# A decoder layer on one Trainium2 core: the softmax division is moved from the probabilities to the output of each pair of heads

## The chip, the core and the metric

The kernel runs on one core of one Trainium2 chip. Five engines work side by side, each through its own queue in order: TensorE (PE, matmuls and transposes), VectorE (DVE), ScalarE (ACT), GpSimd (POOL) and SyncE (SP), which here issues the DMA transfers. The metric is the device time of one execution in microseconds; less is better.

## The reference, cut to what matters

One layer of a hybrid decoder, 512 tokens of width 1024 in float32: a norm, one combined input projection, sparse attention (16 heads of 64) beside a state-space mixer, a gated merge, an output projection, a gated MLP and a last norm. The change touches the attention alone:

```python
def block(args):
    qb, qib, wib, blk = args
    ...
    _, sel = lax.top_k(score, n_sel)
    c_sel = gather(c_kv, sel)
    logits = jnp.einsum("bqhc,bqkc->bhqk", qb, c_sel,
                        preferred_element_type=jnp.float32) * scale
    ...
    logits = jnp.where((dist >= 0)[:, None], logits, -jnp.inf)
    p = jax.nn.softmax(logits, axis=-1).astype(c_sel.dtype)
    return jnp.einsum("bhqk,bqkc->bqhc", p, c_sel)
```

Each query of a head divides its exponentials by their sum. The division may stand before the product with the values or after it, since the sum belongs to the row.

## The kernel before

The kernel keeps float32 accuracy by splitting every operand into a high and a low part (the helper `split`: ACT copies the high part, another engine subtracts to get the low one) and multiplying high by high, high by low and low by high. Weights come in as tiles wr of 512 KB, are split into wh (ACT, L86) and wl (POOL, L87), and two wr buffers are used in turn.

Attention is one loop over h from 0 to 17. A pass writes out, woven together by the helper `weave`: the logits and the softmax of head h, the transposes of the probabilities of head h−1, the product of head h−2 with the values, in every fourth pass the values' projection V (`v_step`), and fillers for PE (projections of the next pairs, gates). Two heads make a pair p, whose output is one tile of 128 partitions, 64 for each head. In a pass:

- `logits` (L720 to L762): a table T of the relative bias is loaded (L726); POOL adds it to the mask into bm (L730, L731, L737), which has one buffer; PE computes the logits of the four query blocks into pl, and DVE adds bm and takes the row maximum (L747) into pr and mx. `soft` lets ACT take the exponentials with the sums in sm (L754), DVE the reciprocals (L756), and DVE scale the four blocks of pr (L759).
- `ptrans` (L764 to L781): PE transposes pr in 128 by 128 blocks (L775, the tile pPT), ACT copies the high part (PTh, L778) and DVE the low part (PTl, L779).
- `pav_` (L785 to L801): PE multiplies with the values V (L794). The result's rows of the head and its low part lie on different halves of the partitions. ACT copies one half into the tile ath (L799), a DMA brings it to the other half into atl (L800), and DVE copies the rest into cr (L801), which has one buffer for all pairs.
- `att_split` (L804 to L808): cr is completed by adding atl (L807), and split into ath (ACT, L86) and atl (L87). POOL does the add and the subtraction for pairs 0 to 5, DVE for 6 and 7.

The order within each engine isn't that of the text: a scheduler moves instructions. In the built program `att_split` of pair p stands on POOL in the pass of the odd head 2p+3, behind the four bm additions. After the loop come the two gates' and the attention's output projections, pga and pao (L105), and the merge; pao needs ath and atl of all eight pairs.

PE's queue, ACT's and DVE's hold the steps of several heads in turn, so a late step holds all that stands behind it on its engine.

Of the kernel before, what the change touches and what calls it, by code (L numbers as in the profile page):

```python
# [9 lines left out]
F32 = mybir.dt.float32  # L10
R32 = mybir.dt.float32r
AF = mybir.ActivationFunctionType
OP = mybir.AluOpType

P = 128
S = 512
# [32 lines left out]
def _body(ctx, tc, x, prm_d, cst_d, nfin_d, wI_d, wX_d, wSO_d, wQ_d, wG_d, wAO_d, wO_d, wUp_d, wDn_d,  # L49
# [18 lines left out]
    def f(t):  # L68
        return t.bitcast(F32)
# [12 lines left out]
    ident = cv("ident")  # L82

    def split(hi, lo, src, lo_eng=None):
        """hi = fp32r(src), lo = fp32r(src - hi)."""
        nc.scalar.activation(hi, src, AF.Copy)  # L86
        (lo_eng or nc.vector).tensor_tensor(lo, src, f(hi), OP.subtract)  # L87

# [10 lines left out]
        return hi, lo  # L99

    def mm3(ps, terms):
        """ps = sum of lhs.T @ rhs over terms of ((lhs_hi, lhs_lo), (rhs_hi, rhs_lo))."""
        seq = [(a[0], b[0]) for a, b in terms] + [(a[0], b[1]) for a, b in terms] + [(a[1], b[0]) for a, b in terms]
        for i, (l, r) in enumerate(seq):
            nc.tensor.matmul(ps, l, r, start=(i == 0), stop=(i == len(seq) - 1))  # L105

    def rsqrt(dst, ss, scale, eps, n, pool):
        """dst = (ss*scale + eps)^-0.5"""
        t = pool.tile([P, n], F32, tag="rsq", name="rsq")
        nc.vector.tensor_scalar(t, ss, scale, eps, OP.mult, OP.add)  # L110
        nc.gpsimd.tensor_tensor(dst, t, mhalf[:, :n], OP.pow)
# [5 lines left out]
            for k in range(KD)]  # L117

    def norm_T(xts, gname, dst, pool, sq, scl):
        """dst = rmsnorm(xts).T in hi and lo; sq and scl: the engine (ACT or DVE) of each block's squares and scaling."""  # L120
        for hf in range(2):
            alloc = mmt if hf == 0 else cht
            ps = [alloc(f"nT{gname}{hf}{i}").rearrange("p (k n) -> p k n", k=2) for i in range(KD // 2)]
            for bb in range(2):
                b = 2 * hf + bb
                xn = pool.tile([P, D], F32, tag="xn", name=f"xn{gname}{b}", bufs=4)
                ss = pool.tile([P, 1], F32, tag="nss", name=f"nss{gname}{b}", bufs=4)
                rs = pool.tile([P, 1], F32, tag="nrs", name=f"nrs{gname}{b}", bufs=4)
                if sq[b] == "v":
                    nc.vector.scalar_tensor_tensor(xn, xts[b], 1.0, xts[b], OP.mult, OP.mult, accum_out=ss)  # L130
                else:
                    nc.scalar.activation(xn, xts[b], AF.Square, accum_out=ss)
                rsqrt(rs, ss, 1.0 / D, EPS, 1, pool)
                if scl[b] == "a":
                    nc.scalar.activation(xn, xts[b], AF.Copy, scale=rs)
                else:
                    nc.vector.tensor_scalar(xn, xts[b], rs, None, OP.mult)
                for k in range(KD):
                    nc.tensor.transpose(ps[k // 2][:, k % 2, bb * P:(bb + 1) * P], xn[:, k * P:(k + 1) * P], ident)
            hs = slice(hf * 256, (hf + 1) * 256)  # L140
            for k in range(KD):
                g = pv(gname, k, k + 1)
                p_ = ps[k // 2][:, k % 2, :]
                nc.scalar.activation(dst[k][0][:, hs], p_, AF.Copy, scale=g)  # L144
                nc.vector.scalar_tensor_tensor(dst[k][1][:, hs], p_, g, f(dst[k][0][:, hs]), OP.mult, OP.subtract)
# [6 lines left out]
    def proj_T(ps, w):  # L152
        mm3(ps, [((w[0][:, k * P:(k + 1) * P], w[1][:, k * P:(k + 1) * P]), actT[k]) for k in range(KD)])

# [1 line left out]
    mid_stack = ExitStack()  # L156
    mid = mid_stack.enter_context(tc.tile_pool(name="mid", bufs=1, side="right"))
    ckvT = (mid.tile([P, S], R32, tag="ckh", name="ckh"), mid.tile([P, S], R32, tag="ckl", name="ckl"))
# [16 lines left out]
    with tc.tile_pool(name="n1", bufs=2) as n1:  # L175
# [15 lines left out]
        nc.sync.dma_start(cs1, cst_d[:, NKEEP:])  # L191
        norm_T(xts, "gmix", actT, n1, "vava", "aavv")

# [1 line left out]
        ps = mmt("pkidx")  # L195
        psc = mmt("pcr")
        for hf in range(2):
# [33 lines left out]
            nc.scalar.activation(ckvT[0], pk, AF.Copy)  # L231
            nc.vector.tensor_tensor(ckvT[1], pk, f(ckvT[0]), OP.subtract)

# [1 line left out]
        dx = dtS.rearrange("p a b -> p (a b)")  # L235
        e = n1.tile([P, 128], F32, tag="sp_e", name="sp_e", bufs=1)
        z = n1.tile([P, 128], F32, tag="sp_z", name="sp_z", bufs=1)
# [35 lines left out]

        latent()

# [1 line left out]
        pu = cht("pu")  # L277
        nc.tensor.matmul(pu[:H, :UW], pv("relb")[:BUCKETS, :], oh, start=True, stop=True)
        us = n1.tile([H, UW], F32, tag="us", name="us", bufs=1)
        nc.vector.tensor_copy(us, pu[:H, :UW])  # L280
        nc.sync.dma_start(uD, us)

# [1 line left out]
    nc.vector.tensor_copy(msk[:, 0:P], cv("maskc"))  # L284
    sds = ExitStack()
    sd = sds.enter_context(tc.tile_pool(name="sd", bufs=2))

    def dup_q(ps, name, tags, pool, scale, bufs):
        """Per head of a pair, its rows hi and lo on both halves of the partitions."""
        out = []  # L290
        for hh in range(2):
            r, o = slice(64 * hh, 64 * hh + 64), slice(64 - 64 * hh, 128 - 64 * hh)
            hi = pool.tile([P, S], R32, tag=tags[2 * hh], name=f"{name}h{hh}", bufs=bufs)
            lo = pool.tile([P, S], R32, tag=tags[2 * hh + 1], name=f"{name}l{hh}", bufs=bufs)
            nc.scalar.activation(hi[r], ps[r], AF.Copy, scale=scale)
            nc.vector.scalar_tensor_tensor(lo[r], ps[r], scale, f(hi[r]), OP.mult, OP.subtract)
            nc.sync.dma_start(f(hi[o]), f(hi[r]))
            nc.sync.dma_start(f(lo[o]), f(lo[r]))
            out.append((hi, lo))
        return out  # L300
# [37 lines left out]
            out += [lambda r=rnd, k=k: r(k=k) for k in range(16)]  # L338
        return out

# [1 line left out]
    def weave(chain, fill):  # L342
        """Emit the chain's (weight, step)s in order, the fillers spread between them by weight."""
        total = sum(w for w, _ in chain) or 1
        acc = done = 0
        for w, step in chain:
# [7 lines left out]
            fill[k]()  # L354

    def proj_steps(name, wsrc, after, parts=2):
        """One column tile of a projection of actT, in emission steps."""
        st = {}

        def seq():  # L360
# [287 lines left out]
    prev[0]()  # L648
    last_trans, so_last = prev[1:]

# [1 line left out]
    attT = []  # L652
    ao_stack = ExitStack()

# [16 lines left out]
            wkv.append((hi, lo))  # L671

    qTs, kTs, Vs, prs, PTs = {}, {}, {}, {}, {}
    KOF = (0, 512, 1024, 896)

    def v_step(qd):
# [44 lines left out]
    def logits(h):  # L721
# [28 lines left out]
        def soft():  # L750
# [3 lines left out]
                nc.scalar.activation(pr[:, o:o + n], pr[:, o:o + n], AF.Exp, bias=mx[:, i:i + 1],  # L754
                                     accum_out=sm[:, i:i + 1])
            nc.vector.reciprocal(sm, sm)  # L756
            for i in range(NB):
                o, n = SEG[i], (i + 1) * P
                nc.vector.tensor_scalar(pr[:, o:o + n], pr[:, o:o + n], sm[:, i:i + 1], None, OP.mult)  # L759
            prs[h] = pr  # L760

        return [lambda i=i: lg(i) for i in range(NB)] + [soft]  # L762
# [20 lines left out]
    crs = {}  # L783

    def pav_(h):  # L785
        """Even heads: [Vh|Vl], odd heads: [Vl|Vh], so that the low part lands on the other half of the partitions."""
        p, hh = h // 2, h % 2
        r, o_ = slice(64 * hh, 64 * hh + 64), slice(64 - 64 * hh, 128 - 64 * hh)
        V, PT = Vs[p // 2], PTs[h]
# [9 lines left out]
        nc.scalar.activation(hi[o_], pav[o_], AF.Copy)  # L799
        nc.sync.dma_start(f(lo[r]), f(hi[o_]))  # L800
        nc.vector.tensor_copy(crs[p][r], pav[r])  # L801

    def att_split(p):
        hi, lo = attT[p]  # L804
        s_ = crs[p]
        eng = nc.vector if p >= 6 else nc.gpsimd
        eng.tensor_tensor(s_, s_, f(lo), OP.add)  # L807
        split(hi, lo, s_, lo_eng=eng)  # L808

    sds.close()  # L810
# [44 lines left out]
        weave(chain, fl)  # L855
    att_split(7)

# [1 line left out]
    at.close()  # L859
    nxs = ExitStack()  # L860
    nx = nxs.enter_context(tc.tile_pool(name="nx", bufs=1, side="right"))
# [15 lines left out]
        split(hi, lo, tg)  # L877
        mg.append((hi, lo))

# [1 line left out]
    x1 = [big.tile([P, D], F32, tag=f"ys{b}", name=f"x1{b}") for b in range(NB)]  # L881
    for b in range(NB):
        nc.sync.dma_start(x1[b], x[b * P:(b + 1) * P, :])
# [120 lines left out]


def _coltile(w):
    """(K, N) -> (N/128, 128, K/128 * 128): per column tile, rows on partitions."""
    k, n = w.shape
    return np.ascontiguousarray(w.reshape(k // P, P, n // P, P).transpose(2, 1, 0, 3)).reshape(n // P, P, k)

# [75 lines left out]
```

## Time and profile before

| | us |
|---|---|
| three runs of the kernel before | 1187.9, 1189.9, 1190.06 |
| their median | 1189.9 |
| span of the profiled execution | 1188.0 |
| attention stage within it, first to last scaling | 525.6 to 677.9 |
| PE busy, share of the span | 1113.1, 94% |
| DVE busy | 705.9, 59% |
| ACT busy | 582.3, 49% |
| POOL busy | 518.0, 44% |
| granted clock of PE, most slices | 0.9 or more of full |

The profiled execution is one more run of the same program; only its span is known, from the first instruction to the last. The runs' times are some microseconds above a span, since they hold what lies around it. The share of busy time is a mean over stages with different limits, so each statement on the change has to be read from the attention stage alone.

### The profile page before, as it was taken

To read this page: it belongs to the slowest core of one execution; us is meant where nothing else is said; L and a number is where in the kernel's file an instruction comes from. 1 tells how busy PE (TensorE), PEld (TensorE's weight loads), DVE (VectorE), ACT (ScalarE), POOL (GpSimd) and SP (SyncE) were. 2 spreads that over 40 slices of the span, in tenths; PEclk is the share of its full clock that TensorE was granted. 3 is DMA by queue.
4 is the path that set the end of the run, shared out by engine and by line. 5 is a ranking of instruction groups with operands and counts; after the bars stand their busy time and mean duration, and the time that the engine had idled before them with its cause. 6 is when DMAs were issued, how large, how long until landed. Compare 5 with 4: busy or idle time off the path is not lost.

```text
span 1188.0 us, 14616 instructions
## 1 busy us (share of the span) xinstructions
PE 1113.1 (94%) x5268; PEld 920.8 (78%) x5268; DVE 705.9 (59%) x1324; ACT 582.3 (49%) x942; POOL 518.0 (44%) x287
## 2 busy tenths in 40 slices
PE   5898996998999889899999899999999999999997
PEld 5677775876887678778878788888888888888885
DVE  5569999998579689368988833305533344330004
ACT  5356464557476555456667633215444444432113
POOL 3324343334524434566566444444444444444442
PEclk9989999999999899999999999999999999999999
DMA  5264322222322231443434133232332222222221
GB/s 186 90 184 143 107 81 80 89 87 74 116 80 83 86 116 59 122 127 107 129 102 125 47 110 123 107 110 86 106 106 90 104 91 99 97 89 107 89 105 73
DMA packets 43306, 122.06 MB, mean 103 GB/s; under 512 B 5393, under 2 KB 9761, under 8 KB 43233
## 3 DMA queue, kind: packets, MB, share of 16 engines
q1 hardware_dynamic: 42656, 120.07, 30.5%
q8 instruction: 42, 0.69, 0.2%
q10 hardware_dynamic: 576, 1.05, 0.2%
q14 instruction: 32, 0.25, 0.1%
HBM read 108.29 MB, written 5.32 MB: 96 GB/s over the span
## 4 chain that ended last, share of the span: by engine, by line
PE 57%; DVE 26%; ACT 5%; issue 3%; POOL 2%; DMA 2%; POOLq 0%; DVEq 0%; ACTq 0%
PE pup L105 20%; PE pdn L947 10%; PE pso L464 5%; PE pao L105 4%; PE pga L105 4%; PE pwo L891 3%; DVE dec L524 3%; DVE u L388 3%; PE pxbc L373 3%; DVE msk L333 2%; DVE dec L527 2%; DVE m L332 2%; DVE pr L747 1%; DVE pr L759 1%; DVE Ml L87 1%
## 5 line engine op out<-in xcount | busy, mean ns | idle before, releaser
L87 POOL TENSOR_TENSOR wl<-wr,wh 128x1024 fp32r<-128x1024 f32 x168 | 409.8, 2440 | 481.4 <-ACT wh L86 260.6
L86 ACT ACTIVATE wh<-wr 128x1024 fp32r<-128x1024 f32 x168 | 177.4, 1057 | 189.1 <-PE pdn L947 80.6
L930 DVE SCALAR_TENSOR_TENSOR fu<-pup,prm,fu 128x511 f32<-128x511 f32 x88 | 65.9, 749 | 124.2 <-ACT fu L928 122.6
L105 PE MATMUL pup<-hTh,wh 128*128 128x512 f32 (+1 forms) x368 | 88.0, 381 | 1.6 <-ACT hTh L144 0.8
L105 PE MATMUL pup<-hTl,wh 128*128 128x512 f32 (+1 forms) x368 | 87.7, 380 | 0.0
L105 PE MATMUL pup<-hTh,wl 128*128 128x512 f32 (+1 forms) x368 | 87.5, 380 | 0.0
L105 PEld LDWEIGHTS pup<-hTh,wh 128*128 128x128 f32 x368 | 67.2, 188 | 15.1 <-ACT hTh L144 1.1
L105 PEld LDWEIGHTS pup<-hTl,wh 128*128 128x128 f32 x368 | 67.2, 188 | 13.1
L105 PEld LDWEIGHTS pup<-hTh,wl 128*128 128x128 f32 x368 | 67.2, 188 | 13.1
L947 PE MATMUL pdn<-wl,fh 128*128 128x512 f32 x176 | 68.6, 390 | 1.2 <-POOL wl L87 1.2
L947 PE MATMUL pdn<-wh,fl 128*128 128x512 f32 x176 | 68.5, 389 | 0.0
L947 PE MATMUL pdn<-wh,fh 128*128 128x512 f32 x176 | 68.4, 390 | 0.0
L974 DVE TENSOR_TENSOR x<-pdn,x 128x512 f32<-128x512 f32 x8 | 5.5, 690 | 104.6 <-PE pdn L947 104.6
L439 PE MATMUL pz<-wh,hTh 128*128 128x512 f32 x128 | 52.4, 409 | 9.9 <-DVE u L388 9.9
L388 DVE SCALAR_TENSOR_TENSOR u<-pxbc,prm,u 128x511 f32<-128x511 f32 (+2 forms) x72 | 53.2, 739 | 9.7 <-ACT u L386 9.3
L373 PE MATMUL pxbc<-hTh,wh 128*128 128x512 f32 x192 | 53.8, 413 | 4.1 <-ACT wh L86 2.9
L524 DVE TENSOR_SCALAR dec<-dec,acS 128x128 f32<-128x128 f32 x128 | 50.6, 450 | 8.9 <-DMA dec<-acD 8.9
L373 PE MATMUL pxbc<-hTh,wl 128*128 128x512 f32 x192 | 51.1, 393 | 0.0
L440 PE MATMUL pz<-wl,hTh 128*128 128x512 f32 x128 | 50.9, 398 | 0.0
L441 PE MATMUL pz<-wh,hTl 128*128 128x512 f32 x128 | 50.9, 398 | 0.0
L373 PE MATMUL pxbc<-hTl,wh 128*128 128x512 f32 x192 | 50.0, 391 | 0.0
L464 PE MATMUL pso<-yTh,wh 128*128 128x512 f32 x128 | 38.7, 426 | 11.4 <-ACT wh L86 7.9
(360 smaller groups left out, 2554.2 us busy)
## 6 DMA issues: line engine op xcount, KB each, us to landing
wr<-wUp SPq DMA_DIRECT2D x44, 512.0 KB, 3.4
wr<-wX SPq DMA_DIRECT2D x40, 512.0 KB, 3.5
wr<-wDn SPq DMA_DIRECT2D x22, 512.0 KB, 3.5
dec<-acD SPq DMA_DIRECT2D x32, 256.0 KB, 3.3
wr<-wSO SPq DMA_DIRECT2D x16, 512.0 KB, 3.5
wr<-wG SPq DMA_DIRECT2D x16, 512.0 KB, 3.6
x<-x SPq DMA_DIRECT2D x8, 512.0 KB, 4.9
wr<-wQ SPq DMA_DIRECT2D x8, 512.0 KB, 3.5
```

Source lines behind the costliest of these rows:

```text
L86: nc.scalar.activation(hi, src, AF.Copy)
L87: (lo_eng or nc.vector).tensor_tensor(lo, src, f(hi), OP.subtract)
L105: nc.tensor.matmul(ps, l, r, start=(i == 0), stop=(i == len(seq) - 1))
L373: nc.tensor.matmul(st["ps"], *st["it"][i], start=(i == 0), stop=(i == 23))
L388: nc.vector.scalar_tensor_tensor(u[:, d:], ps[:, :S - d], pv("cw", o + 3 - d, o + 4 - d), u[:, d:], OP.mult, OP.add)
L439: nc.tensor.matmul(ps, actT[k][0][:, bs], wh[:, ws], start=(k == 0), stop=False)
L440: nc.tensor.matmul(ps, actT[k][0][:, bs], wl[:, ws], start=False, stop=False)
L441: nc.tensor.matmul(ps, actT[k][1][:, bs], wh[:, ws], start=False, stop=(k == KD - 1))
L464: nc.tensor.matmul(ps, *seq[i], start=(i == 0), stop=(i == 11))
L524: nc.vector.tensor_scalar(dec[:, r, :], dec[:, r, :], acS[:, c, r0 + r:r0 + r + 1], 0.0, OP.subtract, OP.min)
L930: nc.vector.scalar_tensor_tensor(u[:, d:], ps[:, :S - d], pv("fw", o + 2 - d, o + 3 - d), u[:, d:], OP.mult, OP.add)
L947: nc.tensor.matmul(po8[b][hf], l[:, bs], r[:, ws], start=(k == 0 and i == 0), stop=(k == NF - 1 and i == 2))
```

## The change

`soft` loses the four scalings. In their place the reciprocal sums of a head, a tile of 128 partitions by 4 blocks, are stored in a new DRAM tensor smD, one row of 512 per head. In `pav_` of an odd head a transfer reads the two rows of the pair from DRAM and spreads each over the 64 partitions of its head, into the tile ath, which is free from the time the transfer from ath to atl has read it until `att_split` writes it. `att_split` multiplies cr by it before the split, on POOL for pairs 0 to 5 and on DVE for 6 and 7. So 64 DVE instructions go, and 16 stores of 2 KB, 8 transfers that write 256 KB each, and 8 multiplications of 128 by 512 come. Otherwise the diff blanks comments and docstrings; line numbers shift by at most three.

```diff
+    smD = dram.tile([H, NB, P], F32, tag="smD", name="smD")
...
             nc.vector.reciprocal(sm, sm)
-            for i in range(NB):
-                o, n = SEG[i], (i + 1) * P
-                nc.vector.tensor_scalar(pr[:, o:o + n], pr[:, o:o + n], sm[:, i:i + 1], None, OP.mult)
+            nc.sync.dma_start(smD[h].rearrange("b p -> p b"), sm)
             prs[h] = pr
...
         nc.sync.dma_start(f(lo[r]), f(hi[o_]))
         nc.vector.tensor_copy(crs[p][r], pav[r])
+        if hh == 1:
+            nc.sync.dma_start(f(hi), bass.AP(tensor=smD.tensor, offset=smD.offset + (h - 1) * S,
+                                             ap=[[S, 2], [0, 64], [1, S]]))
...
         eng = nc.vector if p >= 6 else nc.gpsimd
         eng.tensor_tensor(s_, s_, f(lo), OP.add)
+        eng.tensor_tensor(s_, s_, f(hi), OP.mult)
         split(hi, lo, s_, lo_eng=eng)
```

SP's queue before, at an odd head in the middle of the stage (a number behind a name tells buffers apart; the first row is the transfer from ath to atl of a pair's odd head, the fifth that of the next pair's even head):

```order
L800 DMA atl_4710<-ath_4709 64x512
L726 DMA T_5435<-skD 128x256
L95 DMA wr_5702<-wQ 128x1024
L726 DMA T_5561<-skD 128x256
L800 DMA atl_4712<-ath_4711 64x512
```

The same queue after, at an odd head:

```order
L727 DMA T_5417<-skD 128x256
L799 DMA atl_4705<-ath_4704 64x512
L758 DMA smD<-sm_5074 128x4x1
L802 DMA ath_4704<-smD 128x1x512
L95 DMA wr_5680<-wQ 128x1024
L727 DMA T_5540<-skD 128x256
```

The load of T now stands ahead of a pair's second atl, and between that and the next weight tile stand the store of the current head's reciprocals and the broadcast for the pair.

POOL's queue before, at an odd head, where `att_split` stands:

```order
L730 TENSOR_TENSOR bm_5437<-msk,T_5435 128x128
L731 TENSOR_TENSOR bm_5437<-msk,T_5435 128x3x256
L737 TENSOR_TENSOR bm_5437<-msk,prm 128x128
L737 TENSOR_TENSOR bm_5437<-msk,prm 128x256
L807 TENSOR_TENSOR cr_5265<-cr_5265,atl_4712 128x512
L87 TENSOR_TENSOR atl_4712<-cr_5265,ath_4711 128x512
L87 TENSOR_TENSOR wl_5705<-wr_5702,wh_5704 128x1024
L730 TENSOR_TENSOR bm_5563<-msk,T_5561 128x128
```

The same place after:

```order
L731 TENSOR_TENSOR bm_5419<-msk,T_5417 128x128
L732 TENSOR_TENSOR bm_5419<-msk,T_5417 128x3x256
L738 TENSOR_TENSOR bm_5419<-msk,prm 128x128
L738 TENSOR_TENSOR bm_5419<-msk,prm 128x256
L809 TENSOR_TENSOR cr_5251<-cr_5251,atl_4707 128x512
L87 TENSOR_TENSOR wl_5683<-wr_5680,wh_5682 128x1024
L810 TENSOR_TENSOR cr_5251<-cr_5251,ath_4706 128x512
L87 TENSOR_TENSOR atl_4707<-cr_5251,ath_4706 128x512
L731 TENSOR_TENSOR bm_5542<-msk,T_5540 128x128
```

The wl split has moved ahead of the atl subtraction, and the multiplication stands between the two.

DVE's queue at the end of the stage, before:

```order
L756 RECIPROCAL sm_6248<-sm_6248 128x4
L759 TENSOR_SCALAR pr_6246<-pr_6246,sm_6248 128x128
L759 TENSOR_SCALAR pr_6246<-pr_6246,sm_6248 128x256
L759 TENSOR_SCALAR pr_6246<-pr_6246,sm_6248 128x384
L759 TENSOR_SCALAR pr_6246<-pr_6246,sm_6248 128x512
L718 SCALAR_TENSOR_TENSOR ys_105<-tgs_6339,ys_105 128x512
L87 TENSOR_TENSOR atl_4720<-cr_6206,ath_4719 128x512
L801 COPY cr_6356<-pav_6347 64x512
L779 TENSOR_TENSOR PTl_6346<-pPT_0_6360,PTh_6345 128x512
```

And after:

```order
L757 RECIPROCAL sm_6215<-sm_6215 128x4
L809 TENSOR_TENSOR cr_6176<-cr_6176,atl_4715 128x512
L778 TENSOR_TENSOR PTl_6217<-pPT_2_6286,PTh_6216 128x256
L719 SCALAR_TENSOR_TENSOR ys_105<-tgs_6304,ys_105 128x512
L810 TENSOR_TENSOR cr_6176<-cr_6176,ath_4714 128x512
L778 TENSOR_TENSOR PTl_6312<-pPT_0_6326,PTh_6311 128x512
L778 TENSOR_TENSOR PTl_6312<-pPT_1_6333,PTh_6311 128x512
L778 TENSOR_TENSOR PTl_6312<-pPT_2_6340,PTh_6311 128x256
L87 TENSOR_TENSOR atl_4715<-cr_6176,ath_4714 128x512
```

The multiplication of pair 6 now stands ahead of the three PTl subtractions of the last head, and the scalings ahead of the last transposes are gone.

## Rows read from the trace of the kernel before

**Rows 1.** Windows by cycle: length, busy time and count per engine, PE's clock, DMA
```profile
541.39:561.33 19.94, 19.65 (x107) 16.55 (x106) 16.86 (x41) 13.76 (x32) 13.95 (x13) 1.00 0.38 100
...
603.29:625.52 22.23, 20.98 (x115) 17.46 (x114) 19.68 (x43) 14.73 (x35) 13.76 (x13) 1.00 0.42 124
...
645.24:667.00 21.76, 17.86 (x91) 14.50 (x90) 19.65 (x43) 12.29 (x29) 13.27 (x13) 0.94 0.40 121
```

**Rows 2.** Waits of PE, 515 to 690: total us, times, longest
```profile
PE pav L794 <- DVE mx L747: 4.4, 3, 2.7
PE pPT L775 <- DVE pr L759: 1.7, 1, 1.7
```

**Rows 3.** Groups by line, DVE, 515 to 690: count, busy, mean ns, idle before
```profile
L759 DVE TENSOR_SCALAR pr<-pr,sm 128x128 f32<-128x128 f32 (+1 forms) x64 | 39.0, 660 | 0.5
```

**Rows 4.** Timeline of POOL: start, length, what, idle before with its releaser
```profile
592.30 0.46 POOL L730 TENSOR_TENSOR bm<-msk,T 128x128 f32<-128x128 f32 x1 [4.99 <-DVE mx L747]
...
595.45 1.30 POOL L807 TENSOR_TENSOR cr<-cr,atl 128x512 f32<-128x512 f32 x1
...
612.10 0.46 POOL L730 TENSOR_TENSOR bm<-msk,T 128x128 f32<-128x128 f32 x1 [4.99 <-DVE mx L747]
...
618.72 2.40 POOL L87 TENSOR_TENSOR wl<-wr,wh 128x1024 fp32r<-128x1024 f32 x1
```

**Rows 5.** Timeline of ACT, the same passes
```profile
596.78 0.63 ACT L86 ACTIVATE ath<-cr 128x512 fp32r<-128x512 f32 x1 [1.76 <-POOL cr L807]
...
601.66 0.40 ACT L754 ACTIVATE pr<-pr,mx 128x128 f32<-128x128 f32 x1 [1.61 <-DVE mx L751]
...
603.29 1.09 ACT L778 ACTIVATE PTh<-pPT 128x512 fp32r<-128x512 f32 x2
...
617.60 1.05 ACT L86 ACTIVATE wh<-wr 128x1024 fp32r<-128x1024 f32 x1
```

**Rows 6.** Timeline of DVE, the same passes
```profile
595.05 0.18 DVE L756 RECIPROCAL sm<-sm 128x4 f32<-128x4 f32 x1 [0.25 <-ACT pr L754]
...
606.79 0.40 DVE L759 TENSOR_SCALAR pr<-pr,sm 128x128 f32<-128x128 f32 x1
...
607.95 1.08 DVE L759 TENSOR_SCALAR pr<-pr,sm 128x256 f32<-128x256 f32 x3
```

**Rows 7.** Timeline of SP: the DMA issues
```profile
594.60 0.34 SPq L726 DMA_DIRECT2D T<-skD  x1
601.63 0.33 SPq L95 DMA_DIRECT2D wr<-wQ  x1
...
604.26 0.47 SPq L800 DMA_DIRECT2D atl<-ath  x1
```

**Rows 8.** Line L520, the 32 transfers dec<-acD of 256 KB
```profile
DMA to landing us min/median/max: 3.0/3.3/6.9
```

**Rows 9.** DMA queue, 250.7 to 254.5, one dec alone: packets, MB, share of 16 engines
```profile
q1 hardware_dynamic: 144, 0.26, 19.4%
```

**Rows 10.** DMA queue, 594.5 to 598, one T alone, and its landing
```profile
q1 hardware_dynamic: 144, 0.13, 13.3%
...
T<-skD SPq DMA_DIRECT2D x1, 128.0 KB, 2.1
```

**Rows 11.** Timeline of PE: pav after a long wait, and in the tail
```profile
664.27 1.30 PE L794 MATMUL pav<-PTh,V 128*128 128x512 f32 x4 [2.69 <-DVE mx L747]
...
676.61 0.76 PE L794 MATMUL pav<-PTh,V 128*128 128x512 f32 x4
```

**Rows 12.** Timeline of DVE in the tail
```profile
676.93 0.18 DVE L756 RECIPROCAL sm<-sm 128x4 f32<-128x4 f32 x1
...
686.25 0.69 DVE L807 TENSOR_TENSOR cr<-cr,atl 128x512 f32<-128x512 f32 x1 [2.37 <-DMA atl<-ath]
```

**Rows 13.** Timeline of PE in the tail: end of pav 15, second block of pao
```profile
682.17 0.34 PE L794 MATMUL pav<-PTl,V 128*128 128x256 f32 x2
...
697.48 2.03 PE L105 MATMUL pao<-ath,wh 128*128 128x512 f32 x8
```

## The prediction

> **What bounds the kernel now.** I read the windows of the attention stage first, cut at the same instruction of each cycle (one cycle is one pair of heads, two passes of the loop over h) [rows 1]. A cycle without the V projection lasts 19.7 to 19.9 us and TensorE (PE) is busy 19.65 of it: no slack. A cycle with V lasts 22.2 us and PE is busy 21.0: 1.2 us of slack. The last cycle has 3.9 us of it. DVE is busy 16.9 of 19.9 us, so the scaling that is removed is not simply on the path. Then the waits of PE in the stage [rows 2]: 4.4 us behind the row maxima (the pav matmuls wait for a bank that L747 frees, and L747 stands in DVE's queue behind L759) and 1.7 us directly behind L759. All that removing L759 can give PE is about that, out of 39.0 us of DVE time [rows 3].
>
> Last, the loop that closes a cycle beside PE, along the engines' own times. POOL starts bm of the odd head at 592.30, adds atl to cr at 595.45, and starts the next odd head's bm at 612.10 [rows 4]. Behind the add, ACT splits cr into ath at 596.78, loads wh, and starts the exponentials of the even head at 601.66 [rows 5]. So bm to exponentials is 9.36 us, and exponentials to the next bm 10.44; in the second stretch two pieces of L759 lie on the chain, 0.40 and 1.08 us [rows 6], which leaves 9.0. I call the start of the odd head's bm t0.
>
> **What is removed.** 64 scalings on DVE [rows 3]. Off the path most give nothing; on it they give 1.7 us at the first head (PE's wait goes, next come the logits, which are ready), and some 1.4 us in the chain above. In cycles with V the scalings also stand in front of PE [rows 2], but PE's own work caps such a cycle at 21.0, so at most 1.2 us each.
>
> **What is added on engines.** Six multiplications on POOL at the price of the add beside them, 1.30 us [rows 4], and two on DVE at 0.69 [rows 12]. They alone would fit; what decides is what they wait for. By the order of the changed program POOL runs the add, then a wl split, then the multiplication, and ACT has the split into ath, one wh and then the even head's exponentials in its queue. A late multiplication thus holds ACT's exponentials, POOL's atl subtraction and the next bm, and through them PE's transposes.
>
> **What is added on SP's queue.** Sixteen stores of the reciprocal sums and eight broadcasts. In an odd head the queue holds T, atl, the store, the broadcast, wr, T. T, which stood behind atl before, is issued at t0+2.3, when bm has read its buffer, and atl, now behind it, takes 0.47 us to issue [rows 7] and 2 to 2.5 to land: t0+5.1, and POOL's add, at t0+3.15 before, starts only then. The store waits for the reciprocal of this head. Before, that started at t0+2.75 [rows 6]; the new order of ACT puts ath and two PTh, 0.6 and 1.1 us [rows 5], between the exponentials: t0+4.4. The broadcast overwrites the tile that the atl transfer reads, so it leaves at t0+5.2. Behind it in the queue stand wr and the next T; wr went out at t0+9.3 before [rows 7], when POOL freed its buffer, so holding it till 5.2 costs nothing.
>
> **The price of one broadcast, L.** No row shows such a transfer. The nearest in kind is dec, which also reads one row of DRAM into 128 partitions of 2 KB: it landed 3.0 us after issue at the best, with 144 packets (128 rows and 16 that close the transfer) at 19.4% of 16 engines over 3.8 us, 82 ns a packet [rows 8, 9]. That is the lower bound, with its rows on all 16 engines, 8 rows each. The source pattern of dec has 128 entries outermost; every transfer of the program before has 128, 64 or 16 there. The new one has two (the two heads), each repeated 64 times. If a transfer is dealt out to the engines by its outermost entries, two engines carry 64 rows each: 56 rows more than in dec, 56 × 82 ns = 4.6 us, L = 7.6. The upper bound: T spends 2.1 us on 9 packets of 52 ns [rows 10], so 1.6 us is fixed; dec's other 1.4 us over 8 rows is 175 ns a row, and 64 rows give 1.6 + 11.2 = 12.8. I take the packet time, since with 64 rows queued an engine has less to wait for between them. The store lies ahead of it in the same queues: 512 elements of 4 bytes, each its own packet, 32 an engine, at T's 52 ns 1.7 us, of which 0.8 has passed when the broadcast starts: 0.9 more. **L = 8.5 us**, bounds 3.0 and 12.8.
>
> The Trainium skill, page "DMA: Bandwidth & Descriptors", section "Why a DMA increments its semaphore by 16 and not by 1", says that the number of engines is the largest one up to 16 that divides the outermost size of both patterns, and its section "Rules for kernel authors" warns of just such a short outer dimension. By that rule it is two engines here; all rows here, with 16 closing packets each, agree without testing it. By the same table a non-contiguous last dimension costs one descriptor per element, which is what the store would be; no row here shows one.
>
> **The sum.** The multiplication starts at the later of t0+8.8 (POOL's wl done: 2.4 us behind the add, which ends at t0+6.4) and t0+5.2+L = 13.7. Then 1.30, ath 0.73, wh 1.05, and 9.0 to the next bm: a cycle of 17.3 + L = 25.8 us, if that is over PE's 19.7 or 21.0. Five cycles from 541.39 to 645.24 took 103.85 us and would take 129.0: +25.2.
>
> The tail has three broadcasts behind one another. The one of pair 5 makes the last cycle 17.3 + L instead of 21.76: L − 4.5. That of pair 6 waits in SP's queue for the last reciprocal, at 677.1 [rows 12], 1.3 us earlier without the scaling of the head before; DVE has the multiplication ahead of the last PTl: 677.6 − 1.3 + L, 0.7 for it, 1.8 for PTl and the end of pav, where pav of head 15 ended at 682.5 [rows 13]: L − 3.7. That of pair 7 leaves when the last atl lands, 3.75 us behind pav [rows 12], and then come L, 0.7 and 0.7 till ath is ready; PE has 32 matmuls of 0.23 us to fill 7.4 us of that, and 34 left behind it: 13.1 + L from the end of pav to the end of the second pga, against 15.0 before [rows 13]: L − 1.9. Together 3L − 10.1 = +15.4.
>
> The first head gives −1.7. And PE now idles some 5 us in each cycle. After the only long idle time of the stage before, 2.7 us, the granted clock of that cycle was 0.94, a drop towards the lower of its two levels, and four pav matmuls took 1.30 us instead of 0.76 [rows 1, 11]; eight in each of five cycles: 5 × 1.08 = +5.4, an estimate that may be zero, where PE's steps find slack.
>
> 25.2 + 15.4 − 1.7 + 5.4 = +44.3 on the span of 1188.0. The median of the runs is 1.9 us above that span, which I take for what lies around it: 1188.0 + 44.3 + 1.9 = **1234 us**. With L = 7.6 and no loss of clock it is +31.6, 1222; with L = 12.8 and 9 us for the clock +82, 1272.
>
> **The rivals.** (a) All 16 engines carry the broadcast but find the store's packets ahead of them, or other traffic: L about 5.2. A cycle is 22.5 us: +2.7 for each of three without V, +0.3 for the two with, the tail +5.5, the first head −1.7: +12.4, **1202**. For it: dec itself took from 3.0 to 6.9 us [rows 8]; against: the pattern. (b) All 16 engines and nothing ahead, L = 3.3. The multiplication then waits for POOL's wl alone (up to L = 3.6), and a cycle is 8.8 + 1.3 + 0.7 + 1.05 + 9.0 = 20.9: +1.1 for three, −1.2 for two with V, last cycle −0.8, the rest of the tail +1.0, the first head −1.7: −0.6, **1189**. (c) The other side, faster: as (b), but the chain POOL, ACT, exponentials is not what holds a cycle without V; PE is, which is busy 19.65 of 19.9 us there, and the chain follows it with 1.1 us to spare. Then cycles without V stay, three with V win 1.2 each and the first head 1.7: −5.3, **1185**. It decides only where the broadcast lands by t0+8.8, L of at most 3.6 us; for it speaks PE's busy time, against it that no transfer of 256 KB did better than 3.0 us and that this one has two rows to read from. (d) The change doesn't do what it says: the scalings are gone from the built program and the broadcasts are in it, so only their place in the order could differ, and the order shows it as told.
>
> **How the numbers follow.** 0.72 for the forecast, 0.12 for (a), 0.08 for (b), 0.08 for (c). A difference of 0.2%, 2.4 us, is about what a measurement of this kernel can tell from no change. Faster: (c) and a little of (b), 0.09. Same: most of (b), 0.08. Slower: the rest, 0.83. The range reaches from (a) to well inside the forecast's upper end: 1200 to 1262 leaves out (b), (c) and a broadcast of over some 11 us.
>
> **What would show it.** After the change the time from issue to landing of ath from smD is L: 7 us or more says few engines, 3 to 4 refutes the forecast. The page should show 4-byte packets by the thousand (16 × 512). The POOL multiplication should be preceded by idle time put down to that transfer, some 5 us, six times; cycles should be near 26 us with PE busy still about 20; the tail should have PE waits before pav of head 15 and before the last eighth of pao. If cycles are about 26 us but the wait stands elsewhere (the store, SP's queue), the size was right for a wrong reason. The forecast falls if the transfer lands early, or if the scheduler's order leaves the multiplication room that I have not seen.

## The result and the profile after

The changed kernel takes 1302.5 us (median of four runs, 1301.5 to 1305.1) against 1189.2 us before: 1.096 times the time, 95% interval 1.0935 to 1.098. The direction was forecast, the size was not: +113 us where the prediction had +44, and the time lies above the range's 1262. The profiled execution has a span of 1300.2 us.

The first lines of the page after, busy time and share of each engine and the kinds of DMA packets:

```profile
span 1300.2 us, 14633 instructions
...
PE 1142.7 (88%) x5268; PEld 944.6 (73%) x5268; DVE 667.9 (51%) x1262; ACT 582.1 (45%) x942; POOL 523.3 (40%) x293
...
DMA packets 52792, 124.18 MB, mean 96 GB/s; under 512 B 13856, under 2 KB 18224, under 8 KB 52720
...
PE 53%; DVE 20%; DMA 14%; ACT 5%; issue 3%; POOL 2%; SPq 0%; POOLq 0%; ACTq 0%; DVEq 0%
```

DVE has lost 38 us of work, and PE is idle for 157 us where it was for 75. The page before counted 5393 packets under 512 bytes; 8463 more have come, the 8192 elements of the sixteen stores and the closings of the new transfers. Transfers now hold 14% of the chain that ended last, where they had 2%.

Windows of four cycles after, cut at ACT's first PTh of each pair; the columns are those of [rows 1]:

```profile
576.00:611.45 35.45, 23.30 (x115) 19.53 (x115) 13.60 (x35) 14.57 (x34) 14.74 (x14) 0.84 0.36 75
611.45:648.39 36.94, 21.36 (x103) 17.60 (x103) 12.21 (x33) 13.61 (x32) 14.71 (x14) 0.82 0.46 72
648.39:684.55 36.16, 22.98 (x115) 19.21 (x115) 13.60 (x35) 14.58 (x35) 14.72 (x14) 0.83 0.44 73
684.55:721.50 36.95, 22.20 (x103) 18.31 (x103) 12.29 (x33) 13.61 (x33) 14.71 (x14) 0.78 0.34 72
```

A cycle lasts 35 to 37 us, where it had 19.7 to 22.2 and the prediction 25.8. PE is busy for 21.4 to 23.3 us of it, some 2 us more than before, at a granted clock of 0.78 to 0.84 of full. In one cycle PE works until 635.2, does nothing until 649.2. The stretches before and after that idle time, with the clock in the third column from the end:

```profile
621.50:636.20 14.70, 12.12 (x63) 9.65 (x61) 4.74 (x15) 3.60 (x9) 0.94 (x3) 1.00 0.42 59
...
647.00:656.46 9.46, 7.25 (x27) 6.14 (x28) 6.99 (x18) 6.25 (x16) 5.72 (x6) 0.66 0.75 109
```

It falls from 1.00, the upper of its two levels, to a mean of 0.66 after the long idle stretch.

Who waits, in POOL's list of waits from 505 to 800 (total us, times, longest):

```profile
POOL cr L809 <- DMA atl<-ath: 63.3, 5, 13.9
...
POOL cr L810 <- DMA ath<-smD: 24.5, 6, 4.3
```

The wait that was foreseen is the second, the multiplication waiting for its broadcast. The larger one stands before it and was not foreseen: the add waits for a transfer of 128 KB within the chip, atl, which landed in 2.2 to 3.4 us before. One cycle shows it, POOL's timeline and SP's:

```profile
619.26 0.46 POOL L731 TENSOR_TENSOR bm<-msk,T 128x128 f32<-128x128 f32 x1 [3.48 <-DVE mx L748]
...
636.32 1.26 POOL L809 TENSOR_TENSOR cr<-cr,atl 128x512 f32<-128x512 f32 x1 [13.88 <-DMA atl<-ath]
637.54 2.34 POOL L87 TENSOR_TENSOR wl<-wr,wh 128x1024 fp32r<-128x1024 f32 x1
644.01 1.26 POOL L810 TENSOR_TENSOR cr<-cr,ath 128x512 f32<-128x512 f32 x1 [4.13 <-DMA ath<-smD]
```

```profile
615.79 0.55 SPq L758 DMA_DIRECT2D smD<-sm  x1
...
621.53 0.33 SPq L727 DMA_DIRECT2D T<-skD  x1
621.95 0.46 SPq L799 DMA_DIRECT2D atl<-ath  x1
623.53 0.38 SPq L758 DMA_DIRECT2D smD<-sm  x1
636.22 0.55 SPq L802 DMA_DIRECT2D ath<-smD  x1
```

With t0 = 619.26 the issues stand where the prediction had them: T at t0+2.3, atl at t0+2.7, the store at t0+4.3. But atl lands only at 636.2, 14 us after its issue, and so the broadcast leaves at t0+17.0 instead of t0+5.2. From there on the prediction holds again: the broadcast lands 7.8 us after its issue (636.22 to 644.01) and the multiplication follows at once.

What the 16 DMA engines do meanwhile (three windows; the packets of SP's queue that start in each, their MB, and the time that they took as a share of the 16 engines' time):

```profile
q1 hardware_dynamic: 49, 0.20, 86.1%
```

```profile
q1 hardware_dynamic: 68, 0.00, 0.5%
```

```profile
q1 hardware_dynamic: 71, 0.15, 12.5%
```

The first is 619 to 626, behind the store of the even head. The engines count as 86% busy and move 0.20 MB, 49 packets of nearly all 4 KB, some 2 us for each; in [rows 9], a packet of 2 KB took 82 ns. Packets are open and hardly move. The second is 630 to 637, behind the store of the odd head: 68 packets of under 512 bytes start, all before 630.5, and then none until the end of the window, and yet atl does not land before 636.2. Those 68 are short, 8 ns each by the 0.5%. So the small packets don't fill the time: what follows them is held, and here there isn't even an open packet to see. The third is 637.5 to 640.5, the broadcast alone: 12.5% is two engines of sixteen, at full use, which is what the prediction took from the shape of the source.

Landing times say it again: T after, the store after.

```profile
DMA to landing us min/median/max: 2.2/7.5/13.2
```

```profile
DMA to landing us min/median/max: 9.4/10.6/11.9
```

T took 2.1 us in the median before; the store, 2 KB in all, lands after 9.4 to 11.9 us.

### The profile page after: what moved, and what is told of

The parts are those of the page before. It is cut to its first block, busy times and chain, and to the rows that moved or that the text cites. A ratio compares the mean times of both kernels' runs of the same rounds, so it can differ in the third digit from the quotient of the medians.

```text
span 1300.2 us, 14633 instructions
## 1 busy us (share of the span) xinstructions
PE 1142.7 (88%) x5268; PEld 944.6 (73%) x5268; DVE 667.9 (51%) x1262; ACT 582.1 (45%) x942; POOL 523.3 (40%) x293
## 4 chain that ended last, share of the span: by engine, by line
PE 53%; DVE 20%; DMA 14%; ACT 5%; issue 3%; POOL 2%; SPq 0%; POOLq 0%; ACTq 0%; DVEq 0%
PE pup L105 18%; PE pdn L950 9%; DMA atl<-ath 6%; DMA ath<-smD 5%; PE pso L464 5%; PE pao L105 3%; PE pwo L894 3%; PE pga L105 3%; DVE u L388 3%; DVE dec L524 3%; PE pgs L373 2%; PE pxbc L373 2%; DVE msk L333 2%; DVE dec L527 2%; DVE m L332 1%
## 5 line engine op out<-in xcount | busy, mean ns | idle before, releaser
L800 DVE COPY cr<-pav 64x512 f32<-64x512 f32 x16 | 11.0, 688 | 96.1 <-ACT ath L798 86.2
L373 PE MATMUL pxbc<-hTl,wh 128*128 128x512 f32 x192 | 53.6, 412 | 0.0
```

What stands on the lines that cost most here:

```text
L373: nc.tensor.matmul(st["ps"], *st["it"][i], start=(i == 0), stop=(i == 23))
```

## The experiments

Theory S: the store is at fault. Its 512 elements of 4 bytes hold the DMA engines for some 8 us, sixteen times, and the broadcast costs what the prediction gave it. Theory B: the broadcast on two engines is at fault. Each part was taken away, added alone, and repaired.

**Without the stores.**

```diff
-            nc.sync.dma_start(smD[h].rearrange("b p -> p b"), sm)
...
-            nc.sync.dma_start(f(hi), bass.AP(tensor=smD.tensor, offset=smD.offset + (h - 1) * S,
+            nc.sync.dma_start(f(hi), bass.AP(tensor=acD.tensor, offset=acD.offset,
                                              ap=[[S, 2], [0, 64], [1, S]]))
```

> The changed kernel without the sixteen stores; the broadcast reads two rows of another DRAM tensor instead, in the same pattern, so the division is left out and the rest is as in the changed kernel. Theory S (the store is at fault: its 512 packets of 4 bytes hold the transfers behind them for 6 to 8 us, and the broadcast costs the 7.8 us that the trace shows): the sum of the prediction with L = 7.8 and no packets ahead, 17.6 + 7.5 a cycle, +37, so 1226 us, 1218 to 1236. Theory B (the broadcast on few engines is at fault, since its rows sit in front of everyone's share on these engines): 1280 to 1302.

Measured: 1227.8 us, 1.033 times before (1.029 to 1.037). Two of its cycles, and one multiplication on POOL, whose broadcast was issued at 577.35:

```profile
564.60:589.71 25.11, 22.40 (x115) 19.05 (x115) 15.32 (x35) 14.46 (x35) 14.87 (x14) 0.91 0.35 105
589.71:615.52 25.81, 19.50 (x103) 16.35 (x103) 12.72 (x33) 13.49 (x32) 15.03 (x14) 0.96 0.35 103
```

```profile
577.35 0.56 SPq L801 DMA_DIRECT2D ath<-acD  x1
```

```profile
585.28 1.30 POOL L809 TENSOR_TENSOR cr<-cr,ath 128x512 f32<-128x512 f32 x1 [4.12 <-DMA ath<-acD]
```

The broadcast lands in 7.9 us and a cycle takes 25.1 to 25.8, as the prediction's 17.3 + L has it. So the broadcast, the multiplication and the order cost 39 us, near the forecast's sum, and the stores the other 75. (This kernel's broadcast doesn't wait for the sums of the heads; the kernel with the store repaired, below, where it does, takes the same time.)

**The stores alone**, added to the kernel before, read by nobody.

```diff
             nc.vector.reciprocal(sm, sm)
+            nc.sync.dma_start(smD[h].rearrange("b p -> p b"), sm)
             for i in range(NB):
```

> The kernel before, scalings and all, with the sixteen stores of the reciprocal sums added and nobody reading them. Theory S: T, atl, kT and wr behind a store land 6 to 12 us late, and the ones that POOL and ACT wait for reach PE: 4 to 5 us for each store, 1189 + 70 = about 1260 us, 1235 to 1280. Theory B: a store is 2 KB and nobody waits, 1188 to 1193. A third, W: stores alone hold transfers as in S but the slack of the queue hides it, and it was only the chain of waits (atl landed, then broadcast) that made them costly: 1190 to 1205.

Measured: 1259.4 us, 1.061 (1.057 to 1.064): +71 us, 4.4 us for each store of 2 KB that no instruction reads. Its landing, and PE's longest waits:

```profile
DMA to landing us min/median/max: 8.3/9.5/15.3
```

```profile
PE pl L746 <- issue: 38.0, 5, 8.7
PE pav L796 <- DVE mx L748: 7.2, 2, 6.3
PE pl L746 <- DMA atl<-ath: 6.9, 1, 6.9
```

The profile names no releaser for the longest of them ("issue"), but the logits of L746 read kT, half of which comes by a transfer within the chip that SP issues behind the store. The landing of kT, before and in this run:

```profile
DMA to landing us min/median/max: 2.3/3.4/4.8
```

```profile
DMA to landing us min/median/max: 3.5/12.4/13.7
```

Each of the five waits, and the one put down to atl, ends within 0.2 us of a landing of kT. Theory B falls as an account of the whole loss, and so does the guess that the queue's slack hides the stall: nothing in this kernel waits for the store, but PE waits for transfers that share the engines with it.

**The broadcast repaired, the store kept**, two transfers with 64 entries outermost.

```diff
-            nc.sync.dma_start(f(hi), bass.AP(tensor=smD.tensor, offset=smD.offset + (h - 1) * S,
-                                             ap=[[S, 2], [0, 64], [1, S]]))
+            for t in range(2):
+                nc.sync.dma_start(f(hi[64 * t:64 * t + 64]),
+                                  bass.AP(tensor=smD.tensor, offset=smD.offset + (h - 1 + t) * S,
+                                          ap=[[0, 64], [1, S]]))
```

> The changed kernel with each broadcast written as two transfers, one for each head, whose source has 64 entries outermost; the store stays. Theory S: a broadcast lands in 3 us of its own instead of 7.8, so about 4.6 us less for each of eight pairs: 1302 - 37 = 1265 us, 1255 to 1285. Theory B: 1195 to 1215.

Measured: 1257.6 us, 1.058 (1.055 to 1.061), 45 us less than the change. The gain is a little above the 37 of the expectation; the first half, for the even head, now leaves earlier than the second, which may be why (not tried apart). Behind the stores the halves still land after 2.8 to 9.1 us.

**The store repaired, the broadcast kept**: PE transposes the sums, so that four rows of 512 bytes are stored.

```diff
-            nc.sync.dma_start(smD[h].rearrange("b p -> p b"), sm)
+            pst = cht(f"psm{h}")
+            nc.tensor.transpose(pst[:NB, :P], sm, ident)
+            sr = ap_.tile([NB, P], F32, tag="sr", name=f"sr{h}")
+            nc.vector.tensor_copy(sr, pst[:NB, :P])
+            nc.sync.dma_start(smD[h], sr)
```

> The changed kernel with the sums transposed first by PE (128 by 4 to 4 by 128, one transpose and one small copy on DVE for each head) and stored as four rows of 512 bytes; the broadcast stays as in the changed kernel. Theory S: as without the store, plus 16 small transposes of about 0.1 us: 1228 us, 1218 to 1240. Theory B: 1285 to 1305.

Measured: 1227.4 us, 1.033 (1.030 to 1.036), the same as without any store. It is the form of the store that costs, not that the sums pass through DRAM.

**Both repaired.**

> The changed kernel with both repairs: the sums are transposed by PE and stored as four rows of 512 bytes, and each broadcast is two transfers with 64 entries outermost. Theory S (the rest of the loss was the broadcast's 7.8 us, by the sum of the prediction): a broadcast lands in about 3 us and the multiplication waits for POOL's wl alone, rival (b) of the prediction, 1189 us plus 16 small transposes: 1186 to 1194. If the chain follows PE, rival (c), 1183 to 1187. If the added waits on SP's queue, POOL and ACT cost by themselves, whatever the transfers take: over 1196.

Measured: 1198.6 us, 1.0072 (1.0051 to 1.0094). The 104 us of store and broadcast are gone, and 9 us stay; that is the expectation's last case, in which the added waits and instructions cost by themselves. The landing of its broadcasts, and PE's longest wait:

```profile
DMA to landing us min/median/max: 2.8/2.9/3.0
```

```profile
PE psm L759 <- DVE sm L757: 11.4, 13, 1.6
```

A broadcast of half a tile lands in 2.8 to 3.0 us and no longer binds. PE waits 11.4 us for the reciprocals, before thirteen of its sixteen small transposes: the repair seemed to have a price of its own.

**Without the division**: no scalings, stores, broadcasts or multiplications.

> The changed kernel without the stores, the broadcasts and the multiplications: the division is left out altogether, which bounds what removing the scalings can give. The waits of PE on the scalings go (1.7 and 4.4 us) and little else, since PE has no other idle time to win: 1181 to 1186 us. If the scalings held more than the waits show: below 1180. If the order that the scheduler makes without them is worse: 1188 and over.

Measured: 1185.95 us, 0.9969 (0.9954 to 0.9983). Two cycles:

```profile
559.22:580.50 21.28, 20.28 (x113) 17.13 (x112) 14.62 (x35) 14.68 (x34) 14.14 (x13) 1.00 0.40 113
580.50:600.48 19.98, 19.98 (x110) 17.16 (x109) 13.29 (x33) 13.61 (x32) 12.24 (x13) 1.00 0.39 102
```

This bounds the change: taking 39 us of work from DVE [rows 3] gives 4 us at the most, 2 to 5.5 by the interval. That is little more than can be told here: a kernel below that only adds stores came out at 0.998 of the time before. A cycle with V goes from 22.2 to 21.3, one without stays at PE's 19.7 to 20.0, as the prediction read from [rows 1].

**The store from ACT's queue.**

```diff
-            nc.sync.dma_start(smD[h].rearrange("b p -> p b"), sm)
+            nc.scalar.dma_start(smD[h].rearrange("b p -> p b"), sm)
```

> The changed kernel with the sixteen stores issued from ACT's queue instead of SP's. If the stall sits behind the store in the queue that issued it (the packets of 4 bytes stand in front of SP's later transfers), SP's transfers go past it: about the 1228 us of the kernel without stores plus ACT's issue time of 16 times 0.4 us, 1228 to 1245 us. If it sits in the DMA engines or behind them, which both queues share: 1285 to 1310.

Measured: 1303.4 us, 1.095 (1.092 to 1.098), and the landing of the stores:

```profile
DMA to landing us min/median/max: 9.4/11.8/12.3
```

And that of kT, which stays in SP's queue:

```profile
DMA to landing us min/median/max: 11.2/12.4/14.5
```

Another queue changes nothing: SP's transfers are held by a store that does not stand in SP's queue. The stall sits in what both queues share.

**What makes the store dear.** Four kernels add sixteen dead stores to the kernel before, as above, of other forms. First 128 rows of 16 bytes, the sums as they lie in their tile:

```diff
+    smD = dram.tile([H, P, NB], F32, tag="smD", name="smD")
...
+            nc.sync.dma_start(smD[h], sm)
```

> The kernel before with sixteen stores of the sums that nobody reads, as in the run with stores only, but as 128 rows of 16 bytes instead of 512 elements of 4 bytes: the same 2 KB from the same tile. If the cost goes with the number of packets, 128 instead of 512, a quarter of the 71 us at most and less where the queue has slack: 1190 to 1207 us. If it goes with bytes or with the store as such: 1250 to 1265.

Then 512 pieces of 16 bytes:

```diff
+    smD = dram.tile([H, NB, P, 4], F32, tag="smD", name="smD")
...
+            s4 = ap_.tile([P, NB, 4], F32, tag="s4", name=f"s4{h}")
+            nc.vector.tensor_copy(s4, sm.unsqueeze(2).to_broadcast([P, NB, 4]))
+            nc.sync.dma_start(smD[h].rearrange("b p c -> p b c"), s4)
```

> The kernel before with sixteen stores nobody reads, of 512 pieces of 16 bytes (each sum four times, by a small copy on DVE): four times the bytes of the 4-byte store in as many packets. If the number of packets sets the stall: 1245 to 1270 us. If it is the 4-byte size: 1187 to 1195.

Then 128 elements of 4 bytes, side by side:

```diff
+    smD = dram.tile([H, P, 1], F32, tag="smD", name="smD")
...
+            nc.sync.dma_start(smD[h], sm[:, 0:1])
```

> The kernel before with sixteen stores nobody reads, of 128 elements of 4 bytes (one of the four columns of sums). If each 4-byte write costs the same, a quarter of the stall of about 9 us is left, 2 us a store, 1195 to 1210 us if it shows as it did with 512. If the stall needs many packets behind one another: 1187 to 1192.

And the same 128 elements, 512 bytes apart:

```diff
+    smD = dram.tile([H, P, 128], F32, tag="smD", name="smD")
...
+            nc.sync.dma_start(smD[h][:, 0:1], sm[:, 0:1])
```

> The kernel before with sixteen stores nobody reads, of 128 elements of 4 bytes as in the run before, but 512 bytes apart in DRAM. If the stall comes from writes of several engines that fall side by side into the same few lines of DRAM: gone, 1187 to 1194 us. If a write of 4 bytes is slow wherever it goes: as with 128 side by side, 1228 to 1242.

| sixteen dead stores of | time, us | against before (interval) | landing, min/median/max us |
|---|---|---|---|
| 512 × 4 bytes, side by side | 1259.4 | 1.061 (1.057 to 1.064) | 8.3/9.5/15.3 |
| 128 × 4 bytes, side by side | 1234.95 | 1.040 (1.035 to 1.045) | 6.5/7.8/12.3 |
| 128 × 4 bytes, 512 bytes apart | 1186.2 | 0.998 (0.9956 to 0.9999) | 1.4/1.9/3.4 |
| 128 × 16 bytes, side by side | 1188.3 | 0.9986 (0.997 to 1.0003) | 1.4/2.5/3.9 |
| 512 × 16 bytes, side by side | 1198.8 | 1.007 (1.005 to 1.010) | 2.3/3.1/4.7 |

The landing rows of the two that tell most, side by side and apart:

```profile
DMA to landing us min/median/max: 6.5/7.8/12.3
```

```profile
DMA to landing us min/median/max: 1.4/1.9/3.4
```

The same 128 elements, the same number of packets, the same source: 7.8 us to land if they are neighbours in DRAM, 1.9 if they are not. Neither the number of packets nor the size of 4 bytes alone makes the stall; it is single 4-byte writes that fall next to each other. The expectation that 128 would cost a quarter of 512 missed: they cost 46 us of the 71. The fourfold 16-byte store, with as many pieces as the dear one has, missed both of its ranges: it is far from the 1245 of a stall that goes with the number of pieces, and 4 us above the range without one. Its 10 us hold a copy on DVE for each head besides the store, and were not divided.

**A version without the dear forms**: 128 rows of 16 bytes, two broadcasts per pair with 64 entries outermost, and the multiplication reading the tile with a stride of four.

```diff
-            nc.sync.dma_start(smD[h].rearrange("b p -> p b"), sm)
+            nc.sync.dma_start(smD[h], sm)
...
-        eng.tensor_tensor(s_, s_, f(hi), OP.mult)
+        sv = s_.rearrange("p (b q) -> p b q", b=NB)
+        eng.tensor_tensor(sv, sv, f(hi).rearrange("p (q b) -> p b q", b=NB), OP.mult)
```

> The changed kernel with a store of 128 rows of 16 bytes (the sums as they lie in their tile), each broadcast as two transfers with 64 entries outermost, and the multiplication reading the broadcast tile with a stride of four. No transposes on PE, which waited 11.4 us for the sums in the run with both repairs. Theory S: nothing of the loss is left, 1198.6 - 11.4 = 1187 us, between the kernel without the division (1186) and 1191. If the strided read doubles POOL's multiplication to 2.6 us and it is on the path: 1191 to 1197. If the added waits and instructions cost by themselves: over 1197.

Measured: 1200.6 us, 1.0095 (1.007 to 1.012). No better than with PE's transposes, so those were not what was left. One cycle on POOL:

```profile
595.53 0.46 POOL L731 TENSOR_TENSOR bm<-msk,T 128x128 f32<-128x128 f32 x1 [3.75 <-DVE mx L748]
...
601.69 1.46 POOL L811 TENSOR_TENSOR cr<-cr,atl 128x512 f32<-128x512 f32 x1 [2.97 <-issue]
603.09 2.40 POOL L87 TENSOR_TENSOR wl<-wr,wh 128x1024 fp32r<-128x1024 f32 x1
605.44 1.55 POOL L813 TENSOR_TENSOR cr<-cr,ath 128x512 f32<-128x512 f32 x1
```

The multiplication starts as soon as wl is done and waits for no broadcast. But the add starts at t0+6.2, where it had t0+3.15 before [rows 4] and the prediction 5.1: in the new order atl is issued at t0+1.8 instead of ahead of bm, and in this cycle it lands 4.3 us later, between other transfers.

```profile
atl<-ath SPq DMA_DIRECT2D x1, 128.0 KB, 4.3
```

Then wl and the multiplication follow, and a cycle takes 22.1 to 23.0 us instead of 19.7 to 22.2. That is the chain of the prediction's case (b), not hidden.

**The multiplication taken out of that chain.** Each head's row goes to all 128 partitions right behind its store, into a tile of a later pair that is still free, and DVE multiplies while it empties PSUM.

```diff
+        nc.sync.dma_start(f(t), bass.AP(tensor=smD.tensor, offset=smD.offset + h * S, ap=[[0, P], [1, S]]))
...
-        nc.scalar.activation(hi[o_], pav[o_], AF.Copy)
+        nc.vector.tensor_tensor(hi[o_].rearrange("p (b q) -> p b q", b=NB), pav[o_].rearrange("p (b q) -> p b q", b=NB),
+                                bv[o_], OP.mult)
...
-        nc.vector.tensor_copy(crs[p][r], pav[r])
+        nc.vector.tensor_tensor(crs[p][r].rearrange("p (b q) -> p b q", b=NB), pav[r].rearrange("p (b q) -> p b q", b=NB),
+                                bv[r], OP.mult)
```

> The sums stored as 128 rows of 16 bytes; each head's row is broadcast to all 128 partitions (source pattern with 128 entries outermost) right behind its store, into a tile of a later pair that is still free, two passes before it is needed; DVE multiplies while it takes pav out of PSUM (twice 64 by 512, in place of ACT's copy and its own), so nothing is multiplied or waited for in att_split. If what was left of the loss with 16-byte stores (12 us) was the chain add, wl split, multiplication on POOL behind the late atl, it goes, and the time is near that without division: 1183 to 1189 us. If DVE's two strided multiplications, about 1 us each, hold PTl and PE: 1190 to 1197.

Measured: 1191.3 us, 1.0011 (0.9993 to 1.0029): the time of the kernel before, within what can be told. The 9 to 12 us that were left are gone, so they belonged to the chain on POOL. It isn't the late add that cost them: in this kernel the add starts at t0+5.8 to 8.6, as a rule later still, and in the kernel without the division at t0+4.1 to 7.1, with cycles of 19.7 to 21.3 us. What is gone from the chain in both is the multiplication that stands behind the add and wl. This run also moved the broadcasts and took a copy from ACT, which was not tried apart. The time falls in the second range of the expectation, and the gain of the bound, 4 us, is not reached. A cycle with V shows where it is lost:

```profile
564.68:587.91 23.23, 21.36 (x118) 17.86 (x116) 17.13 (x38) 13.31 (x32) 14.09 (x12) 1.00 0.46 125
```

The two with V take 23.1 and 23.2 us, against 21.3 without the division; those without V take 19.6 to 19.9, as there. The two multiplications take 1.08 to 1.09 us each, against 0.69 for the copy that one of them replaces; whether that is what holds the cycles with V was not followed. No version that keeps the division beat the kernel before.

## Why the prediction went wrong in size

| step | predicted | measured |
|---|---|---|
| rows of the broadcast on few engines, its landing | 2 engines, 7.6 us | 12.5% of 16 engines, 7.8 us |
| T, atl and store issued | t0+2.3, 2.7, 4.4 | t0+2.3, 2.7, 4.3 |
| what the store adds | 0.9 us to each broadcast | 71 us in all when alone, 75 in the change, through every transfer behind it |
| atl landed, broadcast issued | t0+5.1, 5.2 | t0+17.0, 17.0 |
| multiplication starts | t0+13.7 | t0+24.75 |
| cycle | 25.8 us | 35.5 to 37.0; without the stores 24.5 to 25.8 |
| time, with the stores' own share left out | 1227 with L = 7.6 and the clock term, 1222 without that term | 1227.8, four runs from 1224.4 to 1231.6 |
| what removing the scalings can give | a few us, PE being full | 3.9 us |

**What bounds the kernel** was read rightly: without the division it runs 4 us faster, not 39.

**The broadcast** was priced rightly from rows that do not show it. The step that carried it was to read the outermost count of the new pattern beside those of all transfers before, and to take the packet time of [rows 9] rather than the time from issue to landing. The Trainium skill, page "DMA: Bandwidth & Descriptors", section "Rules for kernel authors", says that a short outermost dimension confines a transfer to at most that many engines; the 12.5% agrees.

**The step that failed** is the price of the store. The prediction said: 512 elements, 32 an engine, at T's 52 ns, 1.7 us, of which 0.9 falls on the broadcast. The store landed after 9.4 to 11.9 us instead. Two things were wrong in it. A packet time was carried over from packets of 1 KB read from DRAM to writes of 4 bytes, as one value: the broadcast, which no row showed either, got a bound on both sides, and the store got none. The small packets themselves were even shorter than that, some 8 ns; what was put at nothing is the time from them to the landing, in which the engines are held. And the cost was put on the broadcast alone. What stands behind the store in the engines is every later transfer, and one of them, atl, is what POOL's add waits for: given 2 to 2.5 us to land, it took 14 in the cycle shown. The prediction counted what is queued behind the store on SP, and not on the 16 engines, which serve both SP's and ACT's queue.

Of the signs that the prediction named, three came (the broadcast lands after more than 7 us, 4-byte packets by the thousand, six waits of POOL for it, 24.5 us in all), and the cycle near 26 us came only without the stores.

**The clock term**, 5.4 us, held in kind and not in size. The granted clock is 0.91 to 0.99 in the cycles without the stores and 0.78 to 0.84 with them, and PE's busy time in a cycle rises from 19.7 to as much as 22.2 in cycles without V. But without the stores, where the cycle is the foreseen one, the five cycles last 125.7 us, and 17.3 + L with the measured 7.9 gives 126.0 with no loss of clock: PE, busy 19.5 to 22.5 us of some 25, had room for it. The prediction's sum with L = 7.9 and no clock term is +34 on the span, and the profiled execution of that kernel has +34.9. So the agreement of 1227 with 1227.8 is in part chance, between a term that is not seen and an L that is a little short.

**The other cases.** Case (a), 1202, is a broadcast on 16 engines with the store's packets ahead of it; the kernel with the broadcast repaired and the store kept is that case and took 1257.6, by the same missed price. Case (b), 1189, stands for the kernels with both parts repaired: 1198.6 and 1200.6, about 10 above. A cycle had 20.9 us there, and 21.0 with V; the last of the two took 22.1 to 23.0, with the multiplication at t0+8.2 to 10.4 instead of 8.8, and the one with transposes 21.7 to 22.4 from bm to bm, with the multiplication at t0+8.1 to 9.5, about as assumed. What takes longer behind it in that one was not followed. Case (c), that the chain follows PE with room to spare, falls with them.

## What to carry to other kernels

A new kind of transfer wants a bound on both sides before it is costed, and the upper one is set by what it does to all other transfers, not by its own bytes: sixteen stores of 2 KB cost 71 us here. Columns of a tile that go to DRAM should go as they lie, 16 bytes or more for each partition, and be put in order by the reader, and a broadcast should have its 64 or 128 partitions outermost. Taking work from an engine that is not the bound is worth what the waits on it show, here 4 us of 39.

## What the runs showed of the hardware

- Sixteen stores of 128 single 4-byte elements that are neighbours in DRAM cost 46 us, and the same elements 512 bytes apart cost nothing that can be measured. After a store of 512 of them, in the changed kernel, packets stay open for 7 us and move almost nothing (86% of 16 engines' time for 0.20 MB). Transfers of another queue and within the chip are held too: kT lands after 12.4 us in the median with the stores in ACT's queue, 3.4 before.
- Four times the elements cost 71 us, not 184: a store's landing rises only from 7.8 to 9.5 us in the median.
- Why neighbours stall was not shown. That writes of several engines to the same short stretch of DRAM have to take turns would fit; only the distance was tried, not its threshold, nor the same neighbours written by one engine.
- A transfer whose source has two outermost entries runs on two engines, 64 rows of 2 KB on each, in 7.8 us; one of half the bytes with 64 entries lands in 2.8 to 3.0, and one of the same 256 KB with 128 entries, in the last run, in 3.0 to 4.7.
